# Two half-filled gate weight pieces issued as alternating 64-row matmuls, each into one of two open sums

## The chip, the cores and the metric

The kernel runs on one core of a Trainium2 chip. The metric is device time in microseconds (us) of one execution. PE is TensorE's matmul queue, PEld its weight loads, DVE is VectorE, ACT is ScalarE, POOL is GpSimd, SP is the queue that issues most DMAs.

## The reference, cut to what matters

A two-layer decoder step for 512 prompt tokens and 64 sample tokens (576 columns). Layer 0 is a gated linear recurrence (RG-LRU) over 1536 channels in 16 blocks of 96. The change touches only its two gates, `r` and `ig`, which are block-diagonal products:

```python
xblk = xc.reshape(B, T, N_BLOCKS, BLOCK_W)            # 16 blocks of 96 channels
r  = sigmoid(einsum('btni,nij->btnj', xblk, wa) + ba)
ig = sigmoid(einsum('btni,nij->btnj', xblk, wx) + bx)
a  = exp(-8 * r * softplus(-lam))
u  = sqrt(1 - a*a) * ig * xc
h  = scan(h = a*h + u)
```

Layer 1 is dilated windowed attention and takes most of the time. The change doesn't touch it.

## The kernel before, in words

Channels lie on partitions, tokens along the free dimension, so the 1536 channels are 12 tiles of 128 partitions. The recurrence is worked in four groups (`g` = 0 to 3) of three such tiles (`o` = 0, 1, 2), which are four blocks of 96. Since 96 doesn't divide 128, the block-diagonal weights of a group are laid into six 128x128 pieces (`RUNS`, `gate_w`): three on the diagonal, and three that carry a block across a tile's edge. Two of these crossing pieces, numbers 3 and 5, read input tile 1. Piece 3 has weights only in its upper 64 rows and piece 5 only in its lower 64; the other rows are zero.

Each float32 operand is split into a rounded high part and a low remainder (`XH`, `XL` for inputs, `gH`, `gL` for gate weights, `wH`, `wL` for projection weights, float32r on the chip), and a product is three matmuls: H by XH, H by XL, L by XH. Tokens go in two chunks of 256 and 320 columns. Before, an output tile takes two pieces, so six matmuls in a row into one PSUM bank (L533), and one sigmoid empties the bank (L535). There are 4 groups x 2 gates x 2 chunks x 3 tiles x 6 = 288 of them.

Behind the sigmoids, within a group: `R` is scaled (L536, DVE), `IG` is multiplied by the input (L537, POOL), `A` is the exponential (L538, ACT), then tanh (L539, ACT), `M = A*A` (L540, POOL), `R` from `M` and the tanh (L541, DVE), square root (L542, ACT), `IG` from `R` (L543, DVE), a correction for the sample state (`htmp`, L546, DVE), and the scan (L551, DVE).

Around the gates stand the projections (L183, `project`): per output tile and chunk 24 matmuls, whose weights are split by ACT (`wH`, L149) and DVE (`wL`, L150) into four buffers each. Between them stand pieces of the conditioning of both layers (`ada_part`): L272 takes 512 columns with weights of 32 columns, L245 and L296 finish it after DVE has copied a PSUM bank (`adap`, L242). `sg` (L565, L566) is the second branch's SiLU. Six PSUM banks have the tag `mm`.

The order on each engine is made by a scheduler that walks the code with a model of its own; each engine then runs its list in that order and waits on semaphores. Nothing in the source fixes which matmul stands next to which.

Of the kernel before, what the change touches and what calls it, by code (L numbers as in the profile page):

```python
# [10 lines left out]
AF = mybir.ActivationFunctionType  # L11
# [8 lines left out]
CHUNKS = ((0, 256), (256, 576))  # L20
# [67 lines left out]
def kernel(  # L88
# [9 lines left out]
    V, S, G, T = nc.vector, nc.scalar, nc.gpsimd, nc.tensor  # L98
# [11 lines left out]
    def bank(tag, bufs, name, cols=512):  # L110
        pool = ps if tag == "tp" else sum_pool[0]
        return pool.tile([128, cols], F32, name=name, tag=tag, bufs=bufs)

    mm_bank = lambda: bank("mm", mm_bufs[0], "mm")
# [24 lines left out]
    cb, ba, bx, lamT = (vecT[:, 48 + 12 * i:60 + 12 * i] for i in range(4))  # L139
    ng = vecT[:, 96:112].rearrange("p (l j) -> p l j", l=2)  # L140

    def smp(ap):
        return ap.rearrange("p (b t) -> p b t", t=8)
# [186 lines left out]
    start = ExitStack()  # L330
# [43 lines left out]
    for i in range(5):  # L374
        n = 128 if i < 4 else 64
        S.activation(sqx[0:n], xin[0:n, i], AF.Square, accum_out=ssum[0:n, i:i + 1])
        for kq in range(2):
            a = mm_bank()
# [10 lines left out]
    for c in range(4):  # L389
# [5 lines left out]
        for kt in (2 * c, 2 * c + 1):  # L395
            xn = sp.tile([128, NT], F32, name="xn", tag="xn", bufs=2)
            h = sp.tile([128, NT], F32, name="hmod", tag="hmod", bufs=2)
# [36 lines left out]
    def grp(tag, bufs, dt=F32):  # L434
        return lp.tile([128, 3, NT], dt, name=tag, tag=tag, bufs=bufs)
# [62 lines left out]

    PIECES = (((0, 0), (3, 1)), ((4, 1), (1, None)), ((2, 2), (5, 1)))
    RUNS = ((0, 0, 96, 0, 0), (1, 0, 32, 96, 96), (2, 64, 96, 0, 192), (3, 0, 96, 32, 288),
            (1, 32, 96, 0, 480), (2, 0, 64, 64, 576))
    xM = [lp.tile([128, NT], F32R, name=f"xM{i}") for i in range(2)]
# [3 lines left out]
    def gate_w(w, g):  # L508
        for blk, r0, r1, p0, col in RUNS:
            nc.sync.dma_start(graw[p0:p0 + r1 - r0, col:col + 96], w[0, 4 * g + blk, r0:r1])  # L510
        H = lp.tile([128, 6, 128], F32R, name="gH", tag="gH", bufs=2)
        L = lp.tile([128, 6, 128], F32R, name="gL", tag="gL", bufs=2)
        split(graw.rearrange("p (k c) -> p k c", c=128), H, L)
        return H, L

    def gates(g, xs):
        xc, xH, xL = xs
        R, IG, A, M = grp("R", 1), grp("IG", 1), grp("A", 1), grp("M", 2)
        ws = [gate_w(lru_wa, g), gate_w(lru_wx, g)]
        for t, x in zip(xM, (xH, xL)):  # L520
            G.tensor_copy(t[96:128], x[96:128, 0])
            G.tensor_copy(t[0:32], x[0:32, 2])
        for o in range(3):
            j = 3 * g + o
            for (H, L), dst, bias in zip(ws, (R, IG), (ba, bx)):
                for half in range(2):
                    c0, c1 = CHUNKS[half]
                    pt = mm_bank()[:, :c1 - c0]
                    n = 0
                    for pc, a in PIECES[o]:  # L530
                        h, l = xM if a is None else (xH[:, a], xL[:, a])
                        for w, x in ((H, h), (H, l), (L, h)):
                            T.matmul(pt, w[:, pc], x[:, c0:c1], start=(n == 0), stop=(n == 5))  # L533
                            n += 1
                    S.activation(dst[:, o, c0:c1], pt, AF.Sigmoid, bias=bias[:, j:j + 1])  # L535
            V.tensor_scalar(R[:, o], R[:, o], csp[:, j:j + 1], None, ALU.mult)  # L536
            G.tensor_tensor(IG[:, o], IG[:, o], xc[:, o], ALU.mult)  # L537
        S.activation(A, R, AF.Exp, scale=-1.0)  # L538
        S.activation(R, R, AF.Tanh)  # L539
        G.tensor_tensor(M, A, A, ALU.mult)  # L540
        V.scalar_tensor_tensor(R, M, 1.0, R, ALU.add, ALU.mult)  # L541
        S.activation(R, R, AF.Sqrt)  # L542
        V.tensor_tensor(IG, R, IG, ALU.mult)  # L543
        first = lambda t: t[:, :, NP:].rearrange("p o (b t) -> p o b t", t=8)[:, :, :, 0]
        tmp = lp.tile([128, 3, 8], F32, name="htmp", tag="htmp", bufs=1)
        V.tensor_tensor(tmp, first(A), h0T[:, :, 3 * g:3 * g + 3].rearrange("p b o -> p o b"), ALU.mult)  # L546
        V.tensor_tensor(first(IG), first(IG), tmp, ALU.add)
        V.memset(first(A), 0.0)
        for o in range(3):
            j = 3 * g + o  # L550
            V.tensor_tensor_scan(M[:, o], A[:, o], IG[:, o], 0.0, ALU.mult, ALU.add)  # L551
            G.tensor_copy(stT[:, j, 3:4], M[:, o, NP - 1:NP])
            G.tensor_copy(stT[:, j, 28:36], smp(M[:, o, NP:])[:, :, 7])
        return M
# [20 lines left out]
    x0 = xb_group(0)  # L575
    x1g = xb_group(1)
    m0 = gates(0, x0)
    x2 = xb_group(2)
    m1 = gates(1, x1g)
    yX += gb_group(0, m0)  # L580
    x3 = xb_group(3)
    m2 = gates(2, x2)
    yX += gb_group(1, m1)
    m3 = gates(3, x3)
# [35 lines left out]
    for m in range(8):  # L620
# [3 lines left out]
        if m % 3 == 0:  # L624
            xr = grp("M", 2)
            n = min(3, 8 - m)
# [21 lines left out]
    for q, t in enumerate((acc, sqs[:, 1])):  # L648
        for i in range(5):
            n = 128 if i < 4 else 64  # L650
# [7 lines left out]
    for kt in range(8):  # L658
        tm = grp("M", 2)
        xn1, h = tm[:, 0], tm[:, 1]  # L660
# [16 lines left out]
    cuts, o = [], 0  # L677
# [614 lines left out]
```

## Time and profile before

| what | value |
|---|---|
| three runs | 1206.88 us median, 1202.41 to 1208.57 |
| the profiled execution | 1202.4 us, span 1200.6 us |
| PE busy | 1146.2 us, 95% of the span, 10344 matmuls |
| DVE busy | 845.1 us, 70% |
| ACT busy | 446.5 us, 37% |
| mean granted TensorE clock | 0.981 |

Times in the rows are us from the span's start. A matmul's duration runs from its start to the end of its result and overlaps the next one's; what a matmul costs a full queue is the distance from its start to the next start. A matmul's form, such as 64*128, is rows by columns of the weights.

### The profile page before, as it was taken

The numbers are of one execution on the slowest core, as the hardware profiler recorded it, in microseconds if no ns is written. First come the engines' busy times: TensorE is split into PE (matmuls) and PEld (weight loads), VectorE is DVE, ScalarE is ACT, GpSimd is POOL, SyncE is SP. The second block draws the span as 40 slices with busy tenths as digits, with TensorE's granted clock in tenths as the row PEclk, the third lists the DMA queues.
The fourth block names the chain that finished last, engine by engine and source line by source line (L and its number), as shares of the span: only waits on it lengthen the run. The fifth ranks groups of instructions, "written<-read, shape, count | busy, mean of one in ns | idle before, by whom it ended". The sixth has DMA issues, their size and how long they took to land.

```text
span 1200.6 us, 25763 instructions
## 1 busy us (share of the span) xinstructions
PE 1146.2 (95%) x10344; PEld 1016.4 (85%) x10344; DVE 845.1 (70%) x1611; ACT 446.5 (37%) x896; POOL 215.6 (18%) x299
## 2 busy tenths in 40 slices
PE   5999899999998999899999999999999999999797
PEld 4888889899987988797988897988988988898675
DVE  6789977773338269966687865888763887786545
ACT  4268556743223233233123333233232233233421
POOL 3234534541101101030020020110020200031000
PEclk9899899999998999999999999999999999999899
DMA  9864345444432397481989592989674986576912
GB/s 298 276 182 124 115 141 158 133 124 129 135 114 76 98 249 222 147 243 41 266 223 231 154 242 79 298 226 193 197 176 105 282 224 163 158 222 189 227 43 79
DMA packets 242661, 209.49 MB, mean 174 GB/s; under 512 B 15421, under 2 KB 225053, under 8 KB 242415
## 3 DMA queue, kind: packets, MB, share of 16 engines
q1 hardware_dynamic: 229314, 172.73, 52.8%
q10 hardware_dynamic: 8124, 23.61, 6.7%
q0 software_dynamic: 5104, 11.52, 3.1%
q8 instruction: 81, 1.33, 0.5%
q14 instruction: 38, 0.30, 0.1%
HBM read 188.94 MB, written 18.87 MB: 173 GB/s over the span
## 4 chain that ended last, share of the span: by engine, by line
PE 53%; DMA 6%; DVE 1%; issue 0%; ACT 0%; DVEq 0%; SPq 0%; ACTq 0%
PE mm L183 33%; PE mm L1222 4%; DMA vrow<-in_cache_kv_g_dram 3%; PE pvs L1042 3%; PE pvp L857 2%; PE sc L823 1%; PE tp L780 1%; DMA q<-q2d 1%; PE tp L847 1%; PE sc L828 1%; PE tp L849 1%; DMA wraw<-in_att_w_out_dram 1%; PE pvp L865 1%; PE tp L981 1%; DMA q2d<-qt 1%; PE pvs L1035 0%
## 5 line engine op out<-in xcount | busy, mean ns | idle before, releaser
L183 PE MATMUL mm<-hH,wH 128*128 128x320 f32 (+1 forms) x1552 | 471.0, 303 | 6.2 <-DVE qk L703 4.4
L183 PE MATMUL mm<-hL,wH 128*128 128x320 f32 (+1 forms) x1552 | 465.8, 300 | 2.9 <-issue 2.9
L183 PE MATMUL mm<-hH,wL 128*128 128x320 f32 (+1 forms) x1552 | 465.5, 300 | 0.0
L183 PEld LDWEIGHTS mm<-hH,wH 128*128 128x128 f32 x1552 | 295.6, 190 | 25.7 <-issue 11.6
L183 PEld LDWEIGHTS mm<-hL,wH 128*128 128x128 f32 x1552 | 295.5, 190 | 9.7 <-issue 9.4
L183 PEld LDWEIGHTS mm<-hH,wL 128*128 128x128 f32 x1552 | 295.6, 190 | 5.5 <-issue 5.0
L149 ACT ACTIVATE wH<-wraw 128x512 fp32r<-128x512 f32 (+1 forms) x244 | 148.5, 612 | 294.5 <-PE mm L183 235.1
L150 DVE TENSOR_TENSOR wL<-wraw,wH 128x512 fp32r<-128x512 f32 (+1 forms) x240 | 159.8, 670 | 129.5 <-ACT wH L149 122.6
L842 ACT ACTIVATE p<-p,nm 128x192 f32<-128x192 f32 (+3 forms) x64 | 39.0, 610 | 41.4 <-DVE nm L841 35.3
L783 POOL DMA_DIRECT2D out_dram<-tok x32 | 22.9, 721 | 160.9 <-DVE tok L703 87.4
L955 DVE TENSOR_TENSOR kvc<-kvc,q 128x1024 f32<-128x1024 f32 x32 | 39.0, 1218 | 13.6 <-issue 6.9
L1042 PE MATMUL pvs<-vrow,pT 128*32 128x256 f32 x512 | 44.7, 386 | 2.0 <-DMA vrow<-in_cache_kv_g_dram 2.0
L776 POOL DMA_DIRECT2D out_dram<-kn x8 | 4.5, 567 | 217.1 <-ACT kn L701 129.0
L183 PE MATMUL mm<-YL,wH 128*128 128x256 f32 (+1 forms) x144 | 42.7, 296 | 0.0
L183 PE MATMUL mm<-YH,wH 128*128 128x256 f32 (+1 forms) x144 | 42.6, 296 | 0.0
L183 PE MATMUL mm<-YH,wL 128*128 128x256 f32 (+1 forms) x144 | 42.5, 295 | 0.0
L963 DVE TENSOR_TENSOR pr<-kvc,q 128x1024 f32<-128x1024 f32 x32 | 38.9, 1216 | 2.2 <-DMA q<-q1d 2.2
L963 DVE TENSOR_TENSOR kvc<-kvc,q 128x1024 f32<-128x1024 f32 x32 | 39.1, 1220 | 0.0
L483 DVE SCALAR_TENSOR_TENSOR XC<-xpad,vecT,XC 128x512 f32<-128x512 f32 (+1 forms) x72 | 38.3, 574 | 0.9 <-ACT XC L481 0.9
L956 DVE TENSOR_REDUCE R<-kvc 128x16 f32<-128x1024 f32 x32 | 38.7, 1211 | 0.2
L964 DVE TENSOR_REDUCE R<-kvc 128x16 f32<-128x1024 f32 x32 | 38.7, 1209 | 0.0
L701 ACT ACTIVATE PT<-tp 128x256 f32<-128x256 f32 (+4 forms) x64 | 23.2, 365 | 41.6 <-PE tp L849 21.3
(361 smaller groups left out, 2065.3 us busy)
## 6 DMA issues: line engine op xcount, KB each, us to landing
wraw<-in_att_w_in_dram SPq DMA_DIRECT2D x78, 512.0 KB, 6.7
kvc<-in_cache_kv_g_dram SPq DMA_DIRECT2D x48, 512.0 KB, 5.7
adaw<-in_ada_w_dram SPq DMA_DIRECT2D x64, 256.0 KB, 5.3
kvc<-in_cache_kv_g_dram SPq DMA_DIRECT2D x128, 128.0 KB, 5.4
vrow<-in_cache_kv_g_dram SPq DMA_DIRECT2D x32, 512.0 KB, 8.7
vrow<-in_cache_kv_g_dram SPq DMA_DIRECT2D x64, 256.0 KB, 6.8
wraw<-in_lru_w_in_dram SPq DMA_DIRECT2D x20, 512.0 KB, 4.3
adaw<-in_ada_w_dram SPq DMA_DIRECT2D x64, 128.0 KB, 3.4
```

The source lines that it names most:

```text
L149: S.activation(H, x, AF.Copy)
L150: V.tensor_tensor(L, x, H.bitcast(F32), ALU.subtract)
L183: T.matmul(pt, a[:, k], b[:, c0:c1], start=(i == 0), stop=(i == 3 * n - 1))
L483: V.scalar_tensor_tensor(dst, src, cw[:, k, j:j + 1], dst, ALU.mult, ALU.add)
L842: S.activation(p[:, 0:W], p[:, 0:W], AF.Exp, bias=nm[:, 0:1], accum_out=nm[:, 1:2])
L857: T.matmul(pv[64 * hh:64 * hh + 64, 128 * B:128 * B + 128], tok[0][:, 128 * kb + 64 * hh:128 * kb + 64 * hh + 64], PT0[hh][:, 128 * i:128 ...
L955: V.tensor_tensor(kr, kr, q2[:, i:i + 1].broadcast_to([128, 4, 256]), ALU.mult)
L956: V.tensor_reduce(R2[:, i], kr.rearrange("p j (h d) -> p j h d", h=4), axis=AX.X, op=ALU.add)
L963: V.tensor_tensor(pr, kr, q1[:, c:c + 1].broadcast_to([128, 4, 256]), ALU.mult)
L964: V.tensor_reduce(R1[:, i, :, :, u], pr.rearrange("p j (h d) -> p j h d", h=4), axis=AX.X, op=ALU.add)
L1042: T.matmul(pv[32 * b:32 * b + 32, 0:256], pT[:, 4 * g - 2 + c, 32 * b:32 * b + 32], vr[:, b], start=False, stop=(g == 2 and c == 3), skip_ ...
L1222: T.matmul(pt[0:N], a[:, k, ts], b, start=(n == 0), stop=(n == 23))
```

## The change

Per gate and chunk, two banks are now opened together, for output tiles 0 and 2. Each takes three full matmuls with its diagonal piece (L532). Then the six matmuls with pieces 3 and 5 follow, sliced to the 64 rows that hold weights and written in alternation: upper rows into the first bank, lower rows into the second (L536). A third bank takes tile 1 as before (L541). The three sigmoids come at the end (L545), and the whole of gate R comes ahead of gate IG, where before the tiles were the outer loop. Lines from `V.tensor_scalar(R...)` on are 12 higher after the change (L536 is L548, L541 is L553, L546 is L558, L551 is L563, L565 is L577, L566 is L578).

```diff
-    PIECES = (((0, 0), (3, 1)), ((4, 1), (1, None)), ((2, 2), (5, 1)))
...
+        def terms(a):
+            return ((H, xM[0]), (H, xM[1]), (L, xM[0])) if a is None else \
+                ((H, xH[:, a]), (H, xL[:, a]), (L, xH[:, a]))
+
+        for (H, L), dst, bias in zip(ws, (R, IG), (ba, bx)):
+            for half in range(2):
+                c0, c1 = CHUNKS[half]
+                pts = [mm_bank()[:, :c1 - c0] for _ in range(2)]
+                for pt, o in zip(pts, (0, 2)):
+                    for n, (w, x) in enumerate(terms(o)):
+                        T.matmul(pt, w[:, o], x[:, c0:c1], start=(n == 0), stop=False)
+
+                for n, (w, x) in enumerate(terms(1)):
+                    for pt, pc, rw in zip(pts, (3, 5), (slice(0, 64), slice(64, 128))):
+                        T.matmul(pt, w[rw, pc], x[rw, c0:c1], start=False, stop=(n == 2))
+                pt1 = mm_bank()[:, :c1 - c0]
+                n = 0
+                for pc, a in ((4, 1), (1, None)):
+                    for w, x in terms(a):
+                        T.matmul(pt1, w[:, pc], x[:, c0:c1], start=(n == 0), stop=(n == 5))
+                        n += 1
+                for o, pt in zip((0, 2, 1), pts + [pt1]):
+                    j = 3 * g + o
+                    S.activation(dst[:, o, c0:c1], pt, AF.Sigmoid, bias=bias[:, j:j + 1])
         for o in range(3):
             j = 3 * g + o
-            for (H, L), dst, bias in zip(ws, (R, IG), (ba, bx)):
-                for half in range(2):
-                    c0, c1 = CHUNKS[half]
-                    pt = mm_bank()[:, :c1 - c0]
-                    n = 0
-                    for pc, a in PIECES[o]:
-                        h, l = xM if a is None else (xH[:, a], xL[:, a])
-                        for w, x in ((H, h), (H, l), (L, h)):
-                            T.matmul(pt, w[:, pc], x[:, c0:c1], start=(n == 0), stop=(n == 5))
-                            n += 1
-                    S.activation(dst[:, o, c0:c1], pt, AF.Sigmoid, bias=bias[:, j:j + 1])
             V.tensor_scalar(R[:, o], R[:, o], csp[:, j:j + 1], None, ALU.mult)
             G.tensor_tensor(IG[:, o], IG[:, o], xc[:, o], ALU.mult)
```

What the scheduler made of it differs by group. On PE, at the first gates of group 0 (output, input and weight tiles are named; numbers tell banks apart), before:

```order
L533 MATMUL mm_997<-XH_702,gH_979 128x256
L533 MATMUL mm_997<-XL_703,gH_979 128x256
L533 MATMUL mm_997<-XH_702,gL_980 128x256
L533 MATMUL mm_997<-XH_702,gH_979 128x256
L533 MATMUL mm_997<-XL_703,gH_979 128x256
L533 MATMUL mm_997<-XH_702,gL_980 128x256
L533 MATMUL mm_1005<-XH_702,gH_979 128x320
```

and now, at the same place:

```order
L532 MATMUL mm_997<-XH_702,gH_979 128x256
L532 MATMUL mm_997<-XL_703,gH_979 128x256
L532 MATMUL mm_997<-XH_702,gL_980 128x256
L536 MATMUL mm_997<-XH_702,gH_979 128x256
L536 MATMUL mm_997<-XL_703,gH_979 128x256
L536 MATMUL mm_997<-XH_702,gL_980 128x256
L532 MATMUL mm_998<-XH_702,gH_979 128x256
```

The three 64-row matmuls of bank 997 (L536, upper rows) stand alone; those of its partner, bank 998, come some 15 rows later. On PE in group 1, first gates, now:

```order
L532 MATMUL mm_1435<-XH_759,gL_1417 128x256
L536 MATMUL mm_1434<-XH_759,gH_1416 128x256
L536 MATMUL mm_1435<-XH_759,gH_1416 128x256
L536 MATMUL mm_1434<-XL_760,gH_1416 128x256
L536 MATMUL mm_1435<-XL_760,gH_1416 128x256
L536 MATMUL mm_1434<-XH_759,gL_1417 128x256
L536 MATMUL mm_1435<-XH_759,gL_1417 128x256
L541 MATMUL mm_1448<-XH_759,gH_1416 128x256
```

Here upper (bank 1434) and lower rows (bank 1435) alternate, as the code has it. On DVE in group 1, behind the last scaling of R (`adap_1643` is the copy that L245 waits for on PE), before:

```order
L536 TENSOR_SCALAR R_1406<-R_1406,csp_84 128x576
L150 TENSOR_TENSOR XL_1120<-XC_1118,XH_1119 128x576 x3
L546 TENSOR_TENSOR htmp_1542<-A_1408,h0T_83 128x24
L566 TENSOR_TENSOR sg_1592<-mm_1567,sg_1592 128x256
L150 TENSOR_TENSOR wL_1743<-wraw_1740,wH_1742 128x512
L242 COPY adap_1643<-tp_1389 128x512
L150 TENSOR_TENSOR gL_2154<-graw_695,gH_2153 128x768
```

and now:

```order
L558 TENSOR_TENSOR htmp_1542<-A_1408,h0T_83 128x24
L150 TENSOR_TENSOR XL_1120<-XC_1118,XH_1119 128x576 x3
L560 MEMSET A_1408 128x3x8
L553 SCALAR_TENSOR_TENSOR R_1406<-M_1409,R_1406 128x1728
L150 TENSOR_TENSOR gL_2154<-graw_695,gH_2153 128x768
L578 TENSOR_TENSOR sg_1592<-mm_1567,sg_1592 128x256
L150 TENSOR_TENSOR wL_1743<-wraw_1740,wH_1742 128x512
L242 COPY adap_1643<-tp_1389 128x512
```

The combination of R with M and the tanh (L553, before L541) moved ahead of the copy. ACT there, now:

```order
L550 ACTIVATE A_1408<-R_1406 128x1728
L545 ACT_TABLE_LOAD
L545 ACTIVATE IG_1407<-mm_1506,vecT_80 128x320
L545 ACTIVATE IG_1407<-mm_1507,vecT_80 128x320
L149 ACTIVATE XH_1119<-XC_1118 128x576 x3
L545 ACTIVATE IG_1407<-mm_1520,vecT_80 128x320
L551 ACTIVATE R_1406<-R_1406 128x1728
```

The exponential moved ahead of the last three IG sigmoids of the group; the tanh (L551) stayed behind them.

## Rows read from the trace of the kernel before

**Rows 1.** Timeline, PE, gates of group 0: start, us, then instruction
```profile
84.06 0.31 PE L533 MATMUL mm<-XL,gH 128*128 128x320 f32 x1
84.20 0.31 PE L533 MATMUL mm<-XH,gL 128*128 128x320 f32 x1
...
85.36 0.28 PE L533 MATMUL mm<-XL,gH 128*128 128x256 f32 x1
85.48 0.28 PE L533 MATMUL mm<-XH,gL 128*128 128x256 f32 x1
```

**Rows 2.** Instructions of line L533, weight loads: ns min/median/max
```profile
L533 PEld LDWEIGHTS mm<-XH,gH x80: 186/188/193, 82.6 to 229.9; 128*128 128x128 f32 x80
```

**Rows 3.** Timeline, PE, attention scores, window that holds two 64-row matmuls
```profile
1046.88 0.28 PE L183 MATMUL mm<-hL,wH 128*128 128x256 f32 x1
1047.09 0.49 PE L823 MATMUL sc<-qk 64*128 64x256 f32 x2
```

**Rows 4.** The same place, window that holds all four
```profile
1047.09 0.70 PE L823 MATMUL sc<-qk 64*128 64x256 f32 x4
1047.73 0.26 PE L828 MATMUL sc<-qk 64*32 64x64 f32 x4
```

**Rows 5.** Instructions of line L823 in the window of rows 3
```profile
L823 PE MATMUL sc<-qk x2: 480/480/480, 1047.1 to 1047.1; 64*128 64x256 f32 x2
```

**Rows 6.** Timeline, PE, 32-column weights between 128-column ones, and back
```profile
92.17 1.07 PE L272 MATMUL tp<-adaw,cT 128*32 128x512 f32 x8
93.16 0.39 PE L533 MATMUL mm<-xM,gH 128*128 128x256 f32 x1
93.39 0.28 PE L533 MATMUL mm<-xM,gL 128*128 128x256 f32 x1
```

**Rows 7.** Windows: length, busy us (count) of each engine, clock, DMA
```profile
80.00:97.00 17.00, 15.26 (x110) 12.65 (x109) 17.00 (x39) 12.91 (x27) 6.84 (x10) 1.00 0.60 177
183.00:197.00 14.00, 14.00 (x108) 12.06 (x107) 9.55 (x18) 10.05 (x21) 5.43 (x6) 1.00 0.43 128
143.50:150.30 6.80, 6.75 (x27) 6.76 (x28) 4.29 (x8) 0.63 (x1) 0.86 (x1) 0.50 0.53 151
```

**Rows 8.** Timeline, PE, behind the gates of group 1
```profile
143.55 1.88 PE L245 MATMUL tp<-small,adap 128*128 128x10 f32 x8 [2.73 <-DVE adap L242]
...
145.68 0.47 PE L183 MATMUL mm<-hH,wH 128*128 128x320 f32 x1
145.95 0.47 PE L183 MATMUL mm<-hL,wH 128*128 128x320 f32 x1
```

**Rows 9.** Timeline, DVE, the same stretch
```profile
136.54 5.42 DVE L546 TENSOR_TENSOR htmp<-A,h0T 128x24 f32<-128x24 f32 x1 [0.18 <-ACT A L538]
141.88 0.41 DVE L566 TENSOR_TENSOR sg<-mm,sg 128x256 f32<-128x256 f32 x1
142.22 0.67 DVE L150 TENSOR_TENSOR wL<-wraw,wH 128x512 fp32r<-128x512 f32 x1
142.81 0.68 DVE L242 COPY adap<-tp 128x512 f32<-128x512 f32 x1
143.41 0.94 DVE L150 TENSOR_TENSOR gL<-graw,gH 128x768 fp32r<-128x768 f32 x1
```

**Rows 10.** Timeline, ACT, the same stretch
```profile
133.56 1.28 ACT L538 ACT_TABLE_LOAD   x1
134.85 1.65 ACT L538 ACTIVATE A<-R 128x1728 f32<-128x1728 f32 x1
...
138.10 1.64 ACT L539 ACTIVATE R<-R 128x1728 f32<-128x1728 f32 x1
```

**Rows 11.** Groups of ACT by form, 60 to 245 us: busy, mean ns, idle before
```profile
L149 ACT ACTIVATE XH<-XC 128x576 fp32r<-128x576 f32 x12 | 7.8, 678 | 2.8 <-DVE XC L483 2.4 <-PE mm L533 0.2
...
L535 ACT ACTIVATE IG<-mm,vecT 128x320 f32<-128x320 f32 x12 | 6.3, 527 | 0.8 <-PE mm L533 0.8
```

**Rows 12.** Timeline, DVE, group 2
```profile
209.59 1.95 DVE L541 SCALAR_TENSOR_TENSOR R<-M,R 128x1728 f32<-128x1728 f32 x1
```

## The prediction, made before the changed kernel was run

> **What bounds the kernel now.** I read the windows by stage first, then the timeline of PE inside the gates, then the timelines of the engines around PE's longest wait there.
>
> The gates stand where PE is nearly full. In group 2 it is busy for the whole of its window; in group 0 for 15.26 of 17.00 us, and there DVE is busy for all 17.00 [rows 7]. So PE sets the pace of groups 1 to 3, and in group 0 DVE is as full as PE.
>
> A full matmul there costs 0.12 us with 256 columns (start to start) and 0.147 us with 320 [rows 1]. The weight load behind each lasts 0.188 us [rows 2], longer than the distance between two matmuls, and isn't seen: it runs under the matmul ahead.
>
> One long wait stands behind group 1. PE reaches L245 and waits 2.73 us for DVE's copy, and then runs at a granted clock of 0.50, the lower level, 1.2 GHz, for 6.8 us: its 320-column matmuls stand 0.27 us apart there in place of 0.147 [rows 7, 8]. DVE is late since `htmp`, a tiny operation, took 5.42 us from the end of `A`; `sg`, `wL` and the copy follow it [rows 9]. `A` ended at 136.50 [rows 10], L245 starts at 143.55, which is 7.05 us later.
>
> **What the change does on PE: the gain.** There are as many matmuls, but 96 of the 288 now take 64 rows, 48 upper and 48 lower. If an upper and a lower one run at once, each pair gives back one matmul's distance. No row of before shows this with float32r. The nearest are the attention scores, which alternate rows 0 to 63 and 64 to 127 in float32 (two passes, four matmuls): one alone lasts 0.480 us [rows 5], two together 0.49, so the second starts 0.01 us behind the first [rows 3]; all four are through in 0.70, and the next line starts 0.64 us behind the first [rows 4]. So pairs do run at once, and I take that for float32r too. Bounds per pair: nothing, or the full 0.12 or 0.147.
>
> How many pairs there are is read from the order. In groups 1 to 3 upper and lower rows alternate as written, but for one set that L245 cuts in two: 35 pairs. In group 0 the second bank's diagonal input isn't ready when the first bank could go on, so the scheduler gave each bank its three 64-row matmuls in a row; one pair is left in all of group 0. That makes 17 pairs of 256 columns and 19 of 320: 17 x 0.12 + 19 x 0.147 = 4.8 us.
>
> **The cost: changes of form.** Where the weights' form changes, two things show. The first matmul of the new form starts late: the first 64-row one 0.21 us behind the last full one, in place of 0.12 [rows 3], so 0.09 us. And its weights aren't loaded under the matmul ahead, so it lasts longer and the second starts late: on the way back from 32-column weights, the first matmul lasts 0.39 us in place of 0.28, and the second starts 0.23 us behind it in place of 0.12 [rows 6], so some 0.10 us. Together 0.19 us per change, in each direction: the way back starts just as late (L272 ends at 93.24 and the next starts 0.08 us before that [rows 6], where two full ones overlap by 0.16 [rows 1]).
>
> The order has 22 stretches of 64-row matmuls in the gates. Some border on a change that was there already (L272, L296), so 40 changes are added: 15 in group 0, 7, 10 and 8 in groups 1 to 3. 40 x 0.19 = 7.6 us. The lower bound is nothing where PE would have waited anyway.
>
> The Trainium skill's page "TensorEngine Tiling (Array Packing)", section Key Properties, says that changing the tiling mode drains TensorE, which speaks against this change. The 0.09 us agree with it; it doesn't speak of the bare weight load. By the drain alone the changes would cost 40 x 0.09 = 3.6 us and the sum on PE would be -1.2 us in place of +2.8. The rows decide for the larger.
>
> The skill's page "TensorE: Matmul & The Clock Gate", part 3 (packing small matmuls), says that a weight load overlaps matmuls in flight only when the row group differs. The rows differ: full matmuls, all of one row group, stand 0.12 us apart over loads of 0.188 us [rows 1, 2]. By the rule, the 12 matmuls of group 0 that follow one of their own half would show 0.10 us each, and the sum would be +4.0 us.
>
> **The sum on PE** is 7.6 - 4.8 = +2.8 us: group 0 +2.7 (15 changes, one pair), group 1 -0.3, group 2 +0.4, group 3 -0.1 (rounded). The alternation barely pays for its own changes, and group 0 has the changes without the pairs.
>
> **What becomes of it.** What PE loses in groups 0 and 1 comes ahead of the wait at 143.55, which DVE sets. So there I also go by DVE's new order. `R` was scaled by 133.9 in an order of a DVE that is full, and gate IG no longer stands ahead of `A`: `A` can start at 133.9 in place of 134.85, so some 0.95 us earlier [rows 10]. But DVE now takes `R` with M and the tanh ahead of the copy, and ACT gets to the tanh late. From the end of `A`: a table load 1.28 [rows 10], two IG sigmoids 1.05, three `XH` 2.03, one IG sigmoid 0.53 [rows 11], tanh 1.64 [rows 10], together 6.5; then on DVE `R` 1.95 [rows 12], `gL` 0.94, `sg` 0.41, `wL` 0.67, the copy 0.68 [rows 9], together 4.65. That is 11.2 us in place of 7.05: the copy comes 4.1 - 0.95 = 3.2 us later. In PE's order L245 stands 16 matmuls of 320 columns later, 2.3 us of work that is then done. So the program stands 0.9 us further back when L245 starts, whatever PE lost before. Queued behind that wait on DVE are `sg` (which empties projection banks) and `wL`, the weights of PE's next projections; both come with the copy. With groups 2 and 3 (+0.3) that makes +1.2.
>
> Between +1.2 (the wait swallows all that went before) and +2.8 (nothing is swallowed) I take +2.0 us, as group 0's changes may be hidden in part by its 1.7 us of idle PE. The rest is costed at nothing: the sigmoids and table loads are as many as before; three open banks of six leave three for the projections; ACT no longer holds up gate IG until the scan of the group before is done, a gain that falls ahead of the same wait. Behind the recurrence PE's order is the same to the end. The profiled execution took 1202.4 us, so its like would take 1204.4. It was the fastest of the three shown; their mean is 1206.0 and their median 1206.88, so a median like theirs would be about 1208, which I give.
>
> **Rivals.**
> 1. *The wait behind group 1 vanishes.* `A`, M and `R` come earlier in all groups, and if the tanh comes 2 to 3 us sooner than I add up, PE finds the copy done. It gives back 2.7 us of waiting, and the stretch at the lower clock: some 17 matmuls x 0.12 = 2.1 us. 1202.4 + 2.8 - 4.8 = 1200.4, which is 1204 in the median. Against it: the chain of seven operations on ACT ahead of the tanh.
> 2. *Slower, since pairs don't overlap.* If upper and lower float32r matmuls queue one behind the other, only the changes are left: 1202.4 + 7.6 = 1210.0, some 1214 in the median. It decides if starts in a pair lie 0.12 us apart in place of 0.01. For it: no row shows float32r in pairs.
> 3. *Slower, since DVE waits for the tanh.* In all of groups 1 to 3 the combination stands ahead of `wL` and `sg`. If one more wait of the kind of 143.55 comes of it, with its stretch at the lower clock, 4.8 us are added: 1204.4 + 4.8 = 1209.2, 1213 in the median; two would make 1218. Against it: the chain now starts in the midst of the gates, where PE needs no new projection weights.
> 4. *Faster, changes are free.* If the changes fall where PE would idle, the 4.8 us of the pairs remain: 1197.6, or 1201 in the median. For it, only group 0's idle time.
>
> The Trainium skill's tiling page, section Theoretical Speedup, gives up to 2x for a dimension of 64 or less. Were all 48 pairs to gain that, it would be 24 x 0.12 + 24 x 0.147 = 6.4 us at most, and rival 4 would come to 1196.
>
> **How the numbers follow.** The forecast has 0.58, rival 1 0.14, rival 2 0.08, rival 3 0.15, rival 4 0.05. Runs of the same kernel lie 6 us apart (1202.41 to 1208.57), and 0.5%, or 6 us, is about what can be told from no change. The range goes from rival 4's and rival 1's lower half (1201) to one more wait or the changes alone with some scatter (1215); about 2 in 10 are left out. Faster by over 0.5% needs rival 4 or rival 1 with more than its due, and scatter: 0.08. Slower by over 0.5% is most of rival 2, half of rival 3, and a little of the forecast: 0.18. The rest, 0.74, is within 0.5%.
>
> **What the profile of the changed kernel would show.** Pairs: L536's starts 0.01 us apart within a pair in groups 1 to 3, pairs 0.12 or 0.147 apart; in group 0 single matmuls 0.12 apart (0.22 if the rule on row groups holds). Changes: 0.21 us ahead of each first 64-row matmul and some 0.22 behind it. The wait: L245's eight matmuls behind group 1 still wait 1 to 4 us for the copy, with the clock at 0.50 behind them. It would be wrong if PE's busy time in the gates fell or rose by more than 5 us, or if PE's waits for DVE changed by more than the change on PE itself.

## The result, and the profile after

The changed kernel takes 1220.09 us (median of four runs, 1219.27 to 1222.79), the kernel before 1204.64 us in the same rounds: a ratio of 1.0144, 95% interval 1.0103 to 1.0185. It is slower by 15.5 us by the medians and by some 17 us by the ratio, outside the predicted range and on the side that had a chance of 0.18.

PE's list ahead of the recurrence and behind it is that of before, so I look for the loss in the recurrence. I measure one stage in all kernels: from the first gate matmul of group 0 to the first matmul behind the recurrence's output (L651 before, L663 after). Here is the window of the kernel before over that stage, then the changed kernel's windows: over the window of group 0 [rows 7], over its stretches at the lower clock, and in the last row over the stage (columns as in [rows 7]):

```profile
82.70:352.10 269.40, 260.70 (x1909) 243.31 (x1906) 181.71 (x302) 146.51 (x242) 100.85 (x104) 0.99 0.44 133
```

```profile
80.00:97.00 17.00, 15.09 (x60) 10.87 (x59) 11.20 (x33) 7.88 (x17) 2.67 (x6) 0.62 0.35 98
84.00:97.70 13.70, 13.70 (x51) 10.03 (x52) 7.20 (x23) 5.18 (x12) 1.66 (x4) 0.50 0.28 79
152.30:159.10 6.80, 6.80 (x32) 6.80 (x32) 5.29 (x10) 2.30 (x3) 1.25 (x1) 0.50 0.56 152
217.10:223.90 6.80, 6.11 (x26) 6.11 (x27) 4.77 (x10) 1.80 (x4) 0.86 (x1) 0.50 0.70 232
264.90:268.30 3.40, 3.40 (x8) 1.75 (x9) 2.37 (x4) 0.85 (x3) 1.11 (x1) 0.51 0.28 82
79.00:366.10 287.10, 273.64 (x1911) 247.70 (x1907) 175.25 (x302) 146.57 (x243) 102.07 (x104) 0.95 0.42 125
```

The stage is 17.7 us longer with the same work (in both, 1906 matmuls start in it). PE's idle time in it (length less busy time) went from 8.7 to 13.5 us, which is +4.8. Its busy time rose by 12.9 us, and most of that is the clock: 30.7 us of the stage ran at 0.50, where before it was 6.8 us. At that level a 320-column matmul costs 0.27 us in place of 0.147 [rows 8], so by my estimate 0.45 of such a stretch is lost: 0.45 x 23.9 (30.7 less 6.8) = 10.8 us. What is left, 2.1 us, I put down to the 64-row form itself: the prediction's sum was +2.8.

In group 0, PE's 17 us held 110 matmuls [rows 7]; now 60. DVE, which was busy for all of them, is busy for 11.20. PE's timeline at the place of [rows 1]:

```profile
79.34 0.28 PE L532 MATMUL mm<-XH,gL 128*128 128x256 f32 x1
79.55 0.38 PE L536 MATMUL mm<-XH,gH 64*128 64x256 f32 x1
79.77 0.28 PE L536 MATMUL mm<-XL,gH 64*128 64x256 f32 x1
79.89 0.28 PE L536 MATMUL mm<-XH,gL 64*128 64x256 f32 x1
82.08 0.39 PE L532 MATMUL mm<-XH,gH 128*128 128x256 f32 x1 [1.91 <-ACT XH L149]
...
85.95 0.41 PE L532 MATMUL mm<-XH,gL 128*128 128x256 f32 x1
86.30 0.58 PE L536 MATMUL mm<-XH,gH 64*128 64x256 f32 x1
86.68 0.41 PE L536 MATMUL mm<-XL,gH 64*128 64x256 f32 x1
86.89 0.41 PE L536 MATMUL mm<-XH,gL 64*128 64x256 f32 x1
```

The first change of form shows as predicted: the first 64-row matmul starts 0.21 us behind the last full one, the next 0.22 us behind that in place of 0.12. The row at 82.08 shows what was not foreseen: the new order puts tile 2's first matmul ahead of tile 1's, and tile 2's `XH` isn't there. PE waits 1.91 us and falls to 0.50 at 84.0. From 85.95 on a change takes 0.35 + 0.38 us at that level, where two plain distances would take 0.21 each.

PE's lateness went on to the other engines. What ACT waited for between 79.0 and 101.4 us (line, then us in total, times, longest):

```profile
ACT IG L545 <- PE mm L536: 4.3, 3, 1.7
ACT R L545 <- PE mm L536: 3.2, 2, 2.1
ACT R L545 <- PE mm L541: 2.1, 1, 2.1
```

That is 9.6 us of waiting for the gates' sums, where it was 0.3 us in group 0 before.

The pairs of groups 1 to 3, to be read beside [rows 3] (a row with x2 holds both matmuls of a pair):

```profile
129.18 0.28 PE L532 MATMUL mm<-XH,gL 128*128 128x256 f32 x1
129.39 0.39 PE L536 MATMUL mm<-XH,gH 64*128 64x256 f32 x2
129.61 0.28 PE L536 MATMUL mm<-XL,gH 64*128 64x256 f32 x2
129.73 0.28 PE L536 MATMUL mm<-XH,gL 64*128 64x256 f32 x2
```

Each pair has the span of one matmul: both start within 5 ns, and the next pair starts 0.12 us later.

Behind groups 1, 2 and 3, PE now waits for DVE each time. Of [rows 8] there was only the first. PE's timeline there:

```profile
151.84 1.49 PE L245 MATMUL tp<-small,adap 128*128 128x10 f32 x8 [4.59 <-DVE adap L242]
217.79 1.88 PE L245 MATMUL tp<-small,adap 128*128 128x10 f32 x8 [3.15 <-DVE adap L242]
264.84 1.82 PE L296 MATMUL tp<-adap,small 128*10 128x512 f32 x2 [2.05 <-DVE adap L294]
```

DVE ahead of the first of these waits, to be read beside [rows 9], and POOL under it:

```profile
136.91 0.20 DVE L558 TENSOR_TENSOR htmp<-A,h0T 128x24 f32<-128x24 f32 x1 [1.52 <-ACT A L550]
139.74 4.73 DVE L150 TENSOR_TENSOR XL<-XC,XH 128x576 fp32r<-128x576 f32 x3 [2.63 <-ACT XH L149]
144.43 2.38 DVE L553 SCALAR_TENSOR_TENSOR R<-M,R 128x1728 f32<-128x1728 f32 x1
...
146.74 1.42 DVE L150 TENSOR_TENSOR gL<-graw,gH 128x768 fp32r<-128x768 f32 x1
148.07 0.41 DVE L578 TENSOR_TENSOR sg<-mm,sg 128x256 f32<-128x256 f32 x1
148.41 2.78 DVE L150 TENSOR_TENSOR wL<-wraw,wH 128x512 fp32r<-128x512 f32 x1
151.11 0.68 DVE L242 COPY adap<-tp 128x512 f32<-128x512 f32 x1
```

```profile
147.40 1.27 POOL L521 CAST xM<-XH 32x576 fp32r<-32x576 f32 x1
148.64 1.39 POOL L549 TENSOR_TENSOR IG<-IG,XC 128x576 f32<-128x576 f32 x1
149.99 0.65 POOL L521 CAST xM<-XL 32x576 fp32r<-32x576 f32 x1
```

`htmp` is now short, but `XL`, the combination (L553) and `gL` all stand ahead of the copy. `gL` took 0.94 and `wL` 0.67 us in [rows 9]; now they take 1.42 and 2.78, while POOL works without a gap. ACT there, to be read beside [rows 10]; the exponential no longer has the group's last sigmoids ahead of it, but the tanh still has:

```profile
135.23 1.65 ACT L550 ACTIVATE A<-R 128x1728 f32<-128x1728 f32 x1 [0.74 <-DVE R L548]
...
141.16 1.65 ACT L551 ACTIVATE R<-R 128x1728 f32<-128x1728 f32 x1
```

### The profile page after: what moved, and what is told of

Its sections match the earlier page's. It is cut to its first block, busy times and chain, and to the rows that moved or that the text cites. A ratio compares the mean times of both kernels' runs of the same rounds, so it can differ in the third digit from the quotient of the medians.

```text
span 1220.7 us, 25754 instructions
## 1 busy us (share of the span) xinstructions
PE 1161.9 (95%) x10344; PEld 1020.3 (84%) x10344; DVE 837.0 (69%) x1611; ACT 446.3 (37%) x896; POOL 219.5 (18%) x299
## 3 DMA queue, kind: packets, MB, share of 16 engines
q8 instruction: 81, 1.33, 0.5%
## 4 chain that ended last, share of the span: by engine, by line
PE 51%; DMA 7%; DVE 2%; issue 0%; ACT 0%; SPq 0%; DVEq 0%; ACTq 0%
PE mm L183 32%; PE mm L1234 4%; PE pvs L1054 3%; PE pvp L869 2%; DMA wraw<-in_att_w_out_dram 2%; DMA q<-q2d 2%; DMA vrow<-in_cache_kv_g_dram 2%; PE sc L835 1%; PE tp L792 1%; PE tp L859 1%; PE tp L861 1%; PE sc L840 1%; DMA kvc<-in_cache_kv_g_dram 1%; PE pvp L877 1%; DMA q2d<-qt 1%; PE tp L993 1%
## 5 line engine op out<-in xcount | busy, mean ns | idle before, releaser
L183 PEld LDWEIGHTS mm<-hH,wH 128*128 128x128 f32 x1552 | 297.7, 192 | 27.3 <-issue 12.4
L150 DVE TENSOR_TENSOR wL<-wraw,wH 128x512 fp32r<-128x512 f32 (+1 forms) x240 | 165.3, 692 | 133.1 <-ACT wH L149 127.4
L975 DVE TENSOR_TENSOR pr<-kvc,q 128x1024 f32<-128x1024 f32 x32 | 38.8, 1213 | 3.0 <-DMA q<-q1d 1.6
L976 DVE TENSOR_REDUCE R<-pr 128x16 f32<-128x1024 f32 x32 | 38.5, 1203 | 0.0
```

The source lines that it names most:

```text
L150: V.tensor_tensor(L, x, H.bitcast(F32), ALU.subtract)
L183: T.matmul(pt, a[:, k], b[:, c0:c1], start=(i == 0), stop=(i == 3 * n - 1))
L975: V.tensor_tensor(pr, kr, q1[:, c:c + 1].broadcast_to([128, 4, 256]), ALU.mult)
L976: V.tensor_reduce(R1[:, i, :, :, u], pr.rearrange("p j (h d) -> p j h d", h=4), axis=AX.X, op=ALU.add)
```

## The experiments

Each ratio is to runs of the kernel before on the same chip. It need not be the quotient of the two medians: for `e7` the medians are 1206.90 and 1202.60 us, 0.36% apart, and the ratio is 1.0007. "Idle" is the stage less PE's busy time in it; "at 0.50" sums the stage's stretches at that clock. "Form" is what remains of the change against before: the stage's, less the idle time's, less 0.45 of the lower clock's.

| kernel | ratio (95%) | stage | idle | at 0.50 | form |
|---|---|---|---|---|---|
| before | 1 | 269.4 | 8.7 | 6.8 | |
| after | 1.0144 (1.0103 to 1.0185) | 287.1 | 13.5 | 30.7 | +2.1 |
| after, again (`e13`) | 1.0183 (1.0142 to 1.0224) | 284.5 | 12.2 | 30.7 | +0.8 |
| new order, full rows (`e1`) | 1.0133 (1.0098 to 1.0168) | 276.7 | 12.7 | 13.6 | +0.2 |
| the same, again (`e12`) | 1.0100 (1.0059 to 1.0141) | 277.5 | 12.4 | 17.0 | -0.2 |
| full rows in group 0 only (`e2`) | 1.0129 (1.0093 to 1.0166) | 279.7 | 12.7 | 20.4 | +0.2 |
| no alternation (`e4`) | 1.0128 (1.0094 to 1.0162) | 285.1 | 13.2 | 27.3 | +2.0 |
| before's order, 64 rows (`e5`) | 1.0018 (0.9991 to 1.0045) | 272.3 | 3.0 | 0 | +11.7 |
| exp last (`e6`) | 1.0096 (1.0064 to 1.0128) | 277.0 | 9.3 | 17.0 | +2.4 |
| group 0 as before (`e8`) | 1.0072 (1.0039 to 1.0105) | 276.2 | 12.5 | 13.6 | -0.1 |
| both edits (`e7`) | 1.0007 (0.9979 to 1.0036) | 270.5 | 10.4 | 3.4 | +0.9 |
| both, one stretch (`e9`) | 1.0007 (0.9988 to 1.0026) | 270.2 | 8.7 | 6.8 | +0.8 |
| the same, square on ACT (`e10`) | 1.0003 (0.9976 to 1.0030) | 266.2 | 8.2 | 0 | +0.4 |
| before, square on ACT (`e11`) | 0.9993 (0.9965 to 1.0020) | 265.1 | 7.3 | 0 | +0.2 |

What lies outside the stage varies from profile to profile: from its end to the end of the span it is 848.5 us in before, 854.6 in after, 848.3 in `e8` and 857.6 in `e7`, whose ratio is nonetheless 1.0007. Ahead of the stage the profiles differ too, by up to 4.7 us (78.8 us in `e4`, 83.5 in `e7`). I read nothing from these parts, so the stages are not expected to add up to the ratios.

### Order against form: e1, e2, e4, e5

`e1` keeps the changed kernel's order on every engine and gives the pieces all 128 rows, so nothing pairs. `e2` does so in group 0 only.

```diff
-                    for pt, pc, rw in zip(pts, (3, 5), (slice(0, 64), slice(64, 128))):
+                    for pt, pc, rw in zip(pts, (3, 5), (slice(0, 128), slice(0, 128))):
```

```diff
-                    for pt, pc, rw in zip(pts, (3, 5), (slice(0, 64), slice(64, 128))):
+                    for pt, pc, rw in zip(pts, (3, 5), (slice(0, 64 if g else 128), slice(64 if g else 0, 128))):
```

> The changed kernel with pieces 3 and 5 run over all 128 rows again; every engine's list of instructions is the changed kernel's, row for row, so only the 64-row form is undone. Theory A (the loss lies in the new order: waits behind groups 1 to 3 of 4.6, 3.2 and 2.1 us and the lower clock behind them): those waits stay within 1 us of these, the time is 1210 to 1217 us. Theory B (the loss lies in the 64-row form: 40 changes of form, and the clock that was at 0.50 from 84.0 to 97.7 us in the gates of group 0): the time is 1202 to 1208 us, and the clock in the gates of group 0 is 1.00.

> The changed kernel with full 128-row matmuls in group 0 alone, where the scheduler left the halves unpaired; the order of all engines is the changed kernel's. If the 64-row form of group 0 holds the clock down there (84.0 to 97.7 us), its gates go from 22.4 us to about 14 to 15 us and the time to 1210 to 1213 us. If the clock fell for the 1.9 us wait ahead of them (at 82.1 us), it stays at 0.50 for as long, only the 15 changes go (some 3 to 5 us at the lower clock), and the time is 1215 to 1218 us.

`e4` issues three upper matmuls and then three lower ones:

```diff
-                for n, (w, x) in enumerate(terms(1)):
-                    for pt, pc, rw in zip(pts, (3, 5), (slice(0, 64), slice(64, 128))):
+                for pt, pc, rw in zip(pts, (3, 5), (slice(0, 64), slice(64, 128))):
+                    for n, (w, x) in enumerate(terms(1)):
```

> The changed kernel with the 64-row matmuls of a set written as three upper ones, then three lower ones, in place of alternation; a few rows move on ACT and DVE, none by more than some places. Both theories: pairs at once are all but lost in groups 1 to 3 (one of three may be left where upper and lower meet), 23 to 35 matmuls more in a row, so 3 to 5 us more than the changed kernel: 1223 to 1225 us. If the alternation is worth nothing: 1220 us.

`e5` is the kernel before, order and all, with pieces 3 and 5 cut to 64 rows:

```diff
                         for pc, a in PIECES[o]:
                             h, l = xM if a is None else (xH[:, a], xL[:, a])
+                            rw = {3: slice(0, 64), 5: slice(64, 128)}.get(pc, slice(0, 128))
                             for w, x in ((H, h), (H, l), (L, h)):
-                                T.matmul(pt, w[:, pc], x[:, c0:c1], start=(n == 0), stop=(n == 5))
+                                T.matmul(pt, w[rw, pc], x[rw, c0:c1], start=(n == 0), stop=(n == 5))
```

> The kernel before with pieces 3 and 5 cut to 64 rows and nothing else changed; all engines' orders are those of before. Each bank then has three 64-row matmuls alone, with no pairs: 32 stretches, some 64 changes of form at 0.19 us. Theory B: 12 us more than before at the higher clock, and more if the clock falls in the gates: 1215 to 1230 us. Theory A: the changes are hidden in part by waits, 1205 to 1213 us, and the clock stays at 1.00 in the gates.

The new order with full rows (`e1`) loses 1.33%, 64 rows in the old order (`e5`) 0.18%, within its interval. By the ratios, then, most of the loss is the order's; by the stages it is less than half (`e1` +7.3 us, after +17.7). With four runs each, `e1`, `e2`, `e4` and after can't be told apart by their ratios, which is why `e12` and `e13` repeat two of them below.

Against what was expected: `e1`'s three waits stayed (4.56, 3.29 and 2.22 us), as theory A said, but its median, 1217.56 us, is just above that theory's range, and the clock in group 0 fell for 3.4 us. `e2` is split: group 0 took 15.9 us, as the first reading said, while its 1218.16 us are those of the second. `e5`, at 1205.56 us, came out as theory A said.

`e5` also measures the change of form. The stage has 100 changes of form in it, before has 37; 63 x 0.19 = 12.0 us, and the table's remainder is +11.7. The 0.19 us of the prediction holds. Its windows, over that of group 0 [rows 7] and over the stage:

```profile
80.00:97.00 17.00, 16.40 (x101) 11.76 (x100) 17.00 (x40) 12.19 (x25) 5.99 (x9) 1.00 0.65 189
81.70:354.00 272.30, 269.33 (x1910) 242.27 (x1907) 176.38 (x302) 148.03 (x243) 100.75 (x104) 1.00 0.44 132
```

The kernel hardly shows it: 5.7 us come back as waits that vanish. The wait for the copy is 2.7 of them, since PE now arrives when the copy is done, and the stretch at 0.50 goes with it; the rest are shorter waits in the gates of groups 0 and 1 and for L272's weights. The copy itself ended only 0.8 us later after the first gate matmul (61.7 us, before 60.8), though `A` ended 2.1 us later (56.0 and 53.9): `htmp` took 4.14 us in place of 5.42 and ended, as in the kernel before, within 0.1 us of M on POOL.

`e4` has the stage of after without any alternation in its list, and its trace tells why. PE's timeline, where the list has three upper and then three lower matmuls:

```profile
124.90 0.39 PE L536 MATMUL mm<-XH,gH 64*128 64x256 f32 x2
125.13 0.29 PE L536 MATMUL mm<-XL,gH 64*128 64x256 f32 x2
125.25 0.29 PE L536 MATMUL mm<-XH,gL 64*128 64x256 f32 x2
```

The median, 1218.91 us, says the same as the expectation's second case: the alternation is worth nothing. The six still run as three pairs, 10 ns apart within a pair: each lower matmul runs beside the upper one that stands three places ahead of it. One set that L272 cuts in two shows the list's order:

```profile
127.25 0.42 PE L536 MATMUL mm<-XH,gH 64*128 64x320 f32 x2
127.50 0.30 PE L536 MATMUL mm<-XL,gH 64*128 64x320 f32 x1
127.64 0.31 PE L536 MATMUL mm<-XH,gL 64*128 64x320 f32 x1
128.09 1.27 PE L272 MATMUL tp<-adaw,cT 128*32 128x512 f32 x8
```

Ahead of the cut stand all three of one half and the first of the other, which starts with the first of the three; its other two come alone, from 129.29 on. What counts is that both halves stand in one stretch.

### Undoing the order's two parts: e6, e8, e7

`e6` issues the exponential behind the last gate sigmoid, which on DVE puts the combination back behind the copy in groups 1 and 2:

```diff
-                    S.activation(dst[:, o, c0:c1], pt, AF.Sigmoid, bias=bias[:, j:j + 1])
+                    last = S.activation(dst[:, o, c0:c1], pt, AF.Sigmoid, bias=bias[:, j:j + 1])
...
-        S.activation(A, R, AF.Exp, scale=-1.0)
+        with tc.issue_after(last.ins):
+            S.activation(A, R, AF.Exp, scale=-1.0)
```

> The changed kernel with one edit: the exp that makes `A` is issued behind the last gate IG sigmoid on ACT, as it was before the change. On DVE the combination of `R` with M and the tanh then stands behind `sg`, `wL` and the copy in groups 1 and 2, as before the change; PE's gates keep their 64-row pairs, and group 0 is as in the changed kernel. Theory A (the waits come from DVE's order): L245's waits behind groups 1 and 2 (4.59 and 3.16 us) and L296's behind group 3 (2.05 us) fall to before's 2.7, 0 and 0, and two of the three stretches at the lower clock go; 7 us of waits and some 2 to 4 us of clock come back: 1208 to 1213 us. Theory B (the waits come from what PE lost to the 64-row matmuls and their changes of form, whatever stands first on DVE): the three waits stay within 1 us and the time is that of the changed kernel, 1218 to 1221 us.

`e8` gives group 0 the loop of before and leaves the rest as in after:

```diff
...
+        if g == 0:
+            for o in range(3):
+                j = 3 * g + o
+                for (H, L), dst, bias in zip(ws, (R, IG), (ba, bx)):
...
-        for (H, L), dst, bias in zip(ws, (R, IG), (ba, bx)):
+        for (H, L), dst, bias in zip(ws, (R, IG), (ba, bx)) if g else ():
```

> The changed kernel, but group 0 runs the loop of before (full rows, one sum at a time, tile 1 ahead of tile 2); groups 1 to 3 keep the pairs and DVE's new order. Theory A: group 0's first matmuls take before's 14 us in place of 22, with no wait for XH; but the waits for the copy behind groups 1 to 3 stay (4 to 5, 3 and 2 us) and swallow part of that: 1212 to 1217 us. Theory B: group 0's 15 form changes and its stretch at the lower clock are the whole loss, and the waits are small once they are gone: 1204 to 1209 us.

`e7` has both edits.

> Both edits together: group 0 with before's loop, the exp behind the last IG sigmoid, and the 64-row pairs in groups 1 to 3 (33 pairs in alternation). Theory A: no more than before's one wait of 2.7 us is left, and the gates' own work is within 1 us of before's: 1202 to 1208 us. Theory B (what is lost is lost to the 64-row form): half or more of the loss stays, 1211 to 1218 us.

Each takes back a part, and together they take back all. `e6`'s stage is 10.1 us shorter than after's: its waits behind the groups are 3.09, 1.63 and 0 us in place of 4.59, 3.15 and 2.05, and group 0 keeps its wait and 10.2 us at 0.50. That is larger than theory A's 2.7 and 0. (The edit also moves other rows: on PE the L245 behind group 1 stands 11 matmuls earlier than in after.) Its median, 1216.77 us, is above the 1213 expected. Its interval, 0.64 to 1.28% slower than before, agrees with its stage (+7.6 us, 0.63%) only at the lower end. `e8`'s stage is 10.9 us shorter than after's, and its median, 1212.13 us, is as theory A said; its waits stay, in PE's timeline:

```profile
146.06 1.88 PE L245 MATMUL tp<-small,adap 128*128 128x10 f32 x8 [4.45 <-DVE adap L242]
```

`e7` is level with before, as theory A said, with 33 pairs in its list. Theory B, that the loss belongs to the 64-row form, falls for the pairs of groups 1 to 3: they are there and the loss isn't. For group 0 `e7` can't decide, since it has full rows there.

### Fewer changes, and the tiny operation that takes 4 us: e9, e10, e11

`e9` opens four sums and puts both chunks' 64-row matmuls in one stretch, where the scheduler leaves them together (the sigmoids of tiles 0 and 2 then come ahead of tile 1's matmuls):

```diff
-            for half in range(2):
-                c0, c1 = CHUNKS[half]
+            sets = []
+            for c0, c1 in CHUNKS:
                 pts = [mm_bank()[:, :c1 - c0] for _ in range(2)]
+                sets.append((c0, c1, pts))
...
+            for c0, c1, pts in sets:
+                for n, (w, x) in enumerate(terms(1)):
+                    for pt, pc, rw in zip(pts, (3, 5), (slice(0, 64), slice(64, 128))):
```

> As the kernel with both edits, but in groups 1 to 3 the 64-row matmuls of both column chunks stand in one stretch where the order allows, with four sums open at once, so that there are fewer changes of form per pair. By the sizes read so far (0.19 us a change, 0.12 or 0.147 a pair) it would gain 1 to 2 us over the kernel with both edits if the four open banks hold up nothing: 1201 to 1207 us. If the open banks hold up the projections that run between, new waits for a bank appear in groups 1 to 3, and it is 2 to 6 us slower than the kernel with both edits.

It is level with `e7`. The scheduler cut most of the stretches again: 60 changes of form in the stage against 62. A gain of 1 to 2 us would lie within the interval in any case.

`e10` is `e9` with one line changed, `e11` the kernel before with it:

```diff
-        G.tensor_tensor(M, A, A, ALU.mult)
+        S.activation(M, A, AF.Square)
```

> The kernel with both edits and one stretch, with one more: M = A*A is a square on ACT in place of a multiplication on GpSimd. Theory A says that PE's waits there are DVE's lateness. In that kernel's trace `htmp` (128x24) takes 3.96 us on DVE and ends within 0.1 us of GpSimd's M (3.06 us); without M on GpSimd it should take about 0.2 us, and DVE's new order has the copy right behind `sg`. The copy then comes some 3 us earlier, the waits of 3.15 and 1.70 us behind groups 1 and 2 shrink to under 0.5 us and the lower clock behind them goes: 4 to 7 us less, 1197 to 1202 us, ratio 0.994 to 0.997. If `htmp` is slow for another reason, the waits stay and ACT has 6.6 us more work: 1205 to 1209 us.

> The kernel before with that edit alone (M as a square on ACT), full rows throughout. By theory A its one wait of 2.73 us behind group 1 goes, with the 6.8 us at the lower clock behind it: 3 to 5 us less, 1198 to 1201 us, ratio 0.996 to 0.9975. If the pairs of 64 rows are worth anything, the kernel with pairs and this edit is faster than this one by 1 to 3 us; if not, the two agree. By the other reading (htmp slow of itself) nothing changes: 1203 us.

The mechanism is in part as expected, the gain is not. Timelines of `e9`, DVE and POOL, then of `e10`, DVE, and of `e11`, DVE and POOL:

```profile
136.14 3.96 DVE L579 TENSOR_TENSOR htmp<-A,h0T 128x24 f32<-128x24 f32 x1 [1.65 <-ACT A L571]
```

```profile
134.99 1.42 POOL L569 TENSOR_TENSOR IG<-IG,XC 128x576 f32<-128x576 f32 x1
136.36 0.66 POOL L523 CAST xM<-XL 32x576 fp32r<-32x576 f32 x1
136.99 3.06 POOL L573 TENSOR_TENSOR M<-A 128x1728 f32<-128x1728 f32 x1
```

```profile
136.91 0.79 DVE L579 TENSOR_TENSOR htmp<-A,h0T 128x24 f32<-128x24 f32 x1 [1.18 <-ACT A L571]
...
139.67 0.68 DVE L242 COPY adap<-tp 128x512 f32<-128x512 f32 x1
```

```profile
136.14 1.59 DVE L546 TENSOR_TENSOR htmp<-A,h0T 128x24 f32<-128x24 f32 x1 [0.38 <-ACT A L538]
```

```profile
136.26 1.41 POOL L537 TENSOR_TENSOR IG<-IG,XC 128x576 f32<-128x576 f32 x1
```

In `e9` `htmp` ended at 140.10 and M on POOL at 140.05. Without M on POOL `htmp` takes 0.79 us in `e10` and 1.59 in `e11`, not the 0.2 expected: it now ends 0.07 and 0.06 us behind POOL's IG. The copy starts at 139.67 in `e10` in place of `e9`'s 141.83, and PE's waits for it and the lower clock are gone from the stage of both kernels. Yet PE now waits longer for the weights of L272 from DMA (2.3 and 1.8 us in `e10`, 2.5 in `e11`, 1.55 twice in before), and the ratios are 1.0003 and 0.9993. The one line also made the scheduler move rows on PE, DVE and ACT elsewhere. Both stages are 3 to 4 us shorter than before's in the profile, but no gain shows in the time beyond the noise: no version here beats the kernel before. `e10` has the pairs and `e11` doesn't, and they agree.

### Repeats: e12, e13

> The changed kernel's order with full rows, once more: its first profile had a recurrence stage only 7.3 us longer than before's, while its median was 14.5 us longer. If the order alone makes the whole loss, the ratio is again 1.011 to 1.016. If the 64-row form in group 0 is 6 us of the loss, as the profiles of the stage say, the ratio is 1.005 to 1.009.

> The changed kernel itself, beside the one above on the same chip: ratio 1.012 to 1.017, with the waits of 1.9, 4.6, 3.2 and 2.1 us and a first stretch of gates of 21 to 23 us, if its profile was a typical one.

On one chip the new order with full rows takes 1212.54 us and the changed kernel 1222.75. `e12`'s ratio, 1.0100, lies between its two expectations; `e13`'s, 1.0183, lies above the one for it, with the waits as expected (1.89, 4.60, 3.16 and 2.02 us, first stretch 22.4). So in the new order the 64-row form cost some 10 us more on this chip, where the first runs (`e1` and after) showed 1 to 3; in the old order (`e5`) it cost 0.18%, at most 0.45 by the interval. The stage holds 7.0 us of that, and the table says how: 13.7 us more at 0.50 (6.2 us) and 1 us of its own; 5.2 of the 7.0 us lie in the stage's first 88 matmuls, group 0's (17.2 and 22.4 us). By the stage the order alone makes 7 to 8 of 15 to 18 us, by the ratios 12 to 16 of 17 to 22; how the loss divides between order and form is known no better than that.

## Why the prediction was wrong

**The sum on PE was about right.** Forecast +2.8 us, remainder +2.1 and +0.8 in the two profiles of the changed kernel. The change of form at 0.19 us is confirmed by `e5`; there are 36 pairs, as counted, and their starts lie at most 7 ns apart; group 0's other 64-row matmuls stand alone. Rival 2 (pairs don't overlap) is refuted by the rows at 129.39, rival 4 (changes are free) by the same remainder, which would have been -4.8, and by `e5`'s +11.7. Rival 1, that the wait behind group 1 vanishes, came true only in kernels that don't have the change's order (`e5`, `e10`, `e11`). The prediction's own sign of being wrong appeared: PE's waits for DVE behind the groups rose from 2.7 to 9.8 us, by more than the change on PE itself.

**The pages.** The Trainium skill's page "TensorEngine Tiling (Array Packing)", section Key Properties, states a drain at a change of mode. The late start of 0.09 us agrees with it, but is the smaller half: by that alone `e5` would have lost 63 x 0.09 = 5.7 us, not 11.7. The rule of the Trainium skill's page "TensorE: Matmul & The Clock Gate", part 3, that a load overlaps matmuls in flight only when the row group differs, doesn't hold here: the matmuls at 79.77 and 79.89 are of the same upper half, 0.12 us apart, over loads with medians of 183 to 186 ns. (The same part also allows a load ahead into a background weight buffer, and that the rows don't contradict.)

**The step that failed** is "So the program stands 0.9 us further back when L245 starts, whatever PE lost before". It took DVE's lateness for independent of PE. From the first gate matmul to L245 it is 60.9 us before (82.65 to 143.55) and 72.8 after (79.00 to 151.84), so +11.9; less the 2.3 us of matmuls that moved ahead, +9.6 in place of +0.9. In group 0 DVE lives on what PE gives it, by way of ACT's sigmoids: when PE fell back by 8.2 us there, DVE did too (`A` of group 1 ended 8.3 us later than in `e8`), and nothing was swallowed. `e8`, whose group 0 is before's, has 64.5 us there: +3.6 less 2.3 is +1.3, near the forecast 0.9. Between the two, `e1` and `e12` lost 1.8 and 3.0 us in group 0 and stand +3.5 and +4.7 back: each time group 0's loss and 1.3 to 1.7 us more. So the last clause was wrong, and it is the largest part: of the stage's loss 9.6 us lie ahead of this L245 and 8.0 behind it. That the step's sum on DVE came near is luck: in `e8`, `A` ends 4.3 us earlier than before in place of 0.95, and from its end to the copy's it is 14.9 us in place of 11.2; the two misses cancel.

**Group 0's term** (+2.7 us, "may be hidden in part by its 1.7 us of idle PE") was mis-sized by the wait for `XH` and the clock. The stage's first 88 matmuls took 22.4 us in after, 14.2 in before, 15.9 and 17.2 in `e2` and `e12` (the wait, full rows) and 15.5 in `e5` (64 rows, no wait). Each alone costs 1.3 to 3.0 us, both together 8.2. The prediction says that the second bank's input isn't ready there, but drew only the lost pairs from it: it gave the wait that follows, and the clock behind it, no term.

**Rival 3** is what happened behind groups 2 and 3, where the other 8.0 us of the stage's loss lie: two new waits of 3.15 and 2.05 us, each with its stretch at 0.50. With the combination put back behind the copy (`e6`) they are 1.63 and 0. The prediction named its mechanism and its price (two would make 1218) and gave it too little, by the argument that the chain starts in the midst of the gates. The copy came late all the same: in group 1 it ended 14.9 us behind the end of `A`, where the sum has 11.2. The tanh ended at 142.81, sooner than summed; the combination then waited for `XL` (to 144.47), and from there to the copy's end it was 7.3 us in place of 4.65, with `wL`, `gL` and the combination stretched beside POOL.

## What to carry to other kernels

A rewrite of a loop for one engine also rewrites the scheduler's order on the others: compare the lists, and for each matmul that moved ahead ask when its input is due. A loss ahead of a wait is swallowed only if what sets the wait doesn't itself come later by that loss. Two cases: in `e5` PE came to L245 some 3.5 us later and 2.7 of them went into the wait, as `htmp` and with it the copy ended with POOL's M, only 0.8 us later; in after PE lost 8.2 us in group 0, and the chain to the copy moved with it. And a wait of 2 us that lowered the clock cost far more here where 64-row matmuls followed it (group 0 longer by 6.7 to 9.9 us) than where full ones did (1.7 to 3.0).

## What the runs showed of the hardware

- With group 0's lone 64-row matmuls the clock stood at 0.50 for 13.7 us after a wait of 1.9 us, in both profiles of the changed kernel; it was 17.1 in `e4` and 10.2 in `e6`; with full rows in the same order, behind waits of 2.1 to 2.4 us, it was 3.4 us (`e1`, `e2`) and 6.8 us (`e12`). PE was busy throughout each of these stretches. Without the wait (`e5`) the same 64-row matmuls ran at 1.00. Why the low level lasted longer is not settled; no run varied anything but rows and order.
- Upper and lower 64-row matmuls run side by side even when three of one half are listed ahead of three of the other (`e4`: 10 ns apart).
- A DVE operation of 24 columns took 3.96 us in `e9` (5.42 in [rows 9]) beside POOL and ended with it: POOL worked without a gap from 134.99 to 140.05, `htmp` from 136.14 to 140.10, so it came in between none of POOL's three operations. With M on ACT it took 0.79 (`e10`) and 1.59 us (`e11`), and again ended within 0.1 us of an operation of POOL. The Trainium skill's page "SBUF — State Buffer", section SBUF: two separate sides, says that a DVE operation with two SBUF inputs and a POOL operation that reads SBUF exclude one another, the one that starts first for its whole length. The lock-out agrees with these rows.
